# Hybrid encoder trunk: score maxima from half-height matmuls, two key blocks at a time

## The chip, the cores and the metric

The kernel runs on one core of a Trainium2 chip. The metric is the device time of one execution in microseconds (us), as the median of several runs. TensorE (PE) does the matmuls, VectorE (DVE) and ScalarE (ACT) the element-wise work that reads PSUM, GpSimd (POOL) element-wise work between SBUF tiles, and SyncE (SP) issues the DMAs.

## The reference

One layer of an encoder in float32 is applied to two sequences, a prompt of 256 tokens and a sample of 2048, with the same weights. Its parts:

```python
h = rms_norm(x, norm_mix_g)
q, k, v, x_br, y_br = split(h @ w_in)            # 8 query heads, 2 key/value heads of 64
q, k = rope(rms_norm(q)), rope(rms_norm(k))      # per head
s = (q * 64 ** -0.5) @ k.T                       # every query against every key
attn = softmax(s, axis=-1) @ v                   # each key/value head serves 4 query heads
rec = recurrent_group(x_br, y_br)                # gated linear recurrence, both directions
x = x + concat([attn, rec]) @ w_out
x = x + square(relu(rms_norm(x, norm_mlp_g) @ w_up)) @ w_down
y = rms_norm(x, norm_final_g)
```

The softmax must be that of the exact scores; which number is subtracted before the exponential doesn't change it, so long as nothing overflows.

## The kernel before

**Precision.** Every float32 operand of a large matmul is held as two parts, a high one rounded to the array's float32r format and a low one, the rest. A product is the sum of three matmuls: high by high, high by low, low by high (`mm3`, L201 to L204).

**Stages.** The first stage (to some 600 us) does the input projection for all tokens, the recurrence, and the prompt's attention. The second is the region of the changed code: the sample's attention runs beside the output projection and MLP of the prompt and then of the four sample segments of 512 tokens. The MLP of a segment (`mlp`) is the main stream of matmuls, 12 at a time; after each 12 it calls `tick()`, which lets the attention generator take one step (six steps in five ticks, `faster`). The attention is done at some 2500 us, during the third sample segment; the last segment runs without it.

**Attention.** It works in 32 units: 4 segments x 4 query tiles x 2 key/value heads. A unit has 512 query columns (one head, 512 tokens) and 2048 keys of one key/value head. Three SBUF tiles hold all keys and values of the sample: k1 with the high part of the keys in rows 0 to 63 and the low part in rows 64 to 127, k2 with the high part again in rows 0 to 63 and a row of ones as row 64, and vv. A unit has two query tiles: qd holds the high part of the queries twice (rows 0 to 63 and 64 to 127), ql the low part in rows 0 to 63 and, as row 64, minus the maximum of each query. So two matmuls give the scores minus the maxima: k1 by qd (L974: high by high plus low by high) and k2 by ql (L975: high by low, and ones by minus the maxima).

`guard(u)` prepares unit u. It issues the loads of qd for unit u + 1 (`load_q`, three buffers) and of ql for unit u (`load_ql`, two buffers), and then finds the maxima: for each of 4 key blocks of 512 and each of 4 query blocks of 128, one matmul of qd by k1 (L870, with the queries as the weights, so that a row of the result is a query) and one VectorE reduction over it (L871), one of these per step. A reduction over the 4 blocks (L876), four transposes with one column of weights (L880) and a ScalarE copy (L881) then put minus the maxima into row 64 of ql. The maxima's results, the transposes and the sums of `finish` share two PSUM buffers (tag aux).

`values(u)` takes 16 chunks of 128 keys: scores (L974, L975) into one of two PSUM buffers, exp (L982), a copy to the high part (L984), the low part (L986, VectorE), a running sum (L990, POOL), and three chunks later the products with the values (L979, L980). `attention()` runs `guard(u + 1)` beside `values(u)`.

**Order.** No engine's order is written out by hand. The instructions of the whole program are traced first, and a planner then places them on each engine by a simulated timeline: of what is ready it takes what was traced first. The order that it finds is fixed in the program; an engine waits at the head of its order. Where an instruction waits in the plan, later ones go ahead of it.

Of the kernel before, what the change touches and what calls it, by code (L numbers as in the profile page):

```python
# [12 lines left out]
F32 = mybir.dt.float32  # L13
FR = mybir.dt.float32r
AF = mybir.ActivationFunctionType
ALU = mybir.AluOpType
AX = mybir.AxisListType
PSUM = bass.MemoryType.PSUM

P = 128  # L20
# [3 lines left out]
DEC = 2048  # L24
T = SEQ + DEC
NT = 512
# [25 lines left out]
def f32(ap):  # L52
    return ap.bitcast(F32)
# [23 lines left out]
def trunk(ctx, tc, xT, w_in, w_out, w_up, w_down, vecs, wa, wx, cos, sin, outT):  # L77
    nc = tc.nc
    mm = nc.tensor.matmul
    act = nc.scalar.activation  # L80
# [8 lines left out]
    def loadr(out, src):  # L89

        load(f32(out), src)
# [7 lines left out]
    def dtile(shape, name):  # L99
        return dram.tile(shape, F32, name=name, tag=name)  # L100

    def ctile(shape, name, dt=F32):
        return const.tile(shape, dt, name=name, tag=name)
# [15 lines left out]
    k_d = {r: dtile([2, P, n], f"k_d{r}") for r, n in (("p", SEQ), ("s", DEC))}  # L119
# [8 lines left out]
    class WStream:  # L128
# [16 lines left out]
        def load(self, end):  # L145
            while self.at[0] < end:
                i = self.at[0]
                hi, _, first = self.saved[i]
                if first or hi is None:
                    self.f[i] = self._tile("wf", F32, i)  # L150
                    load(self.f[i], self.srcs[i])
                self.at[0] += 1
# [70 lines left out]
    for key in keys:  # L223
        if key[0] == "i":
            w, e = w_in[key[1]], key[2]
        elif key[0] == "o":
            w, e = w_out[key[1]], key[2]
        else:
            (kind, g, f), e = key
            w = w_up[g * G + f] if kind == "u" else w_down[g, f]  # L230
# [6 lines left out]
    nb = (len(srcs) - n1) // len(segs)  # L237
# [10 lines left out]
    for i in range(2):  # L248
        o = ctile([P, P], f"ones_{i}", FR)
# [7 lines left out]
    def load_keys(r, k1, k2, o, n):  # L257
        for k, i in ((k1[0:64], 0), (k1[64:128], 1), (k2[0:64], 0)):
            loadr(k[:, :, o:o + n], k_d[r][i, :, o:o + n].rearrange("(a p) n -> p a n", a=2))
# [12 lines left out]
    with ExitStack() as c1:  # L272
# [461 lines left out]
        for hf in range(2):  # L734
            for ii, m in enumerate((order_s, order_t)[hf]):
                i = len(order_p) + hf * len(order_s) + ii
# [67 lines left out]
    with ExitStack() as c2:  # L804
        banks[0] = itertools.cycle(("m0", "m1"))
        sm = c2.enter_context(tc.tile_pool(name="m2", bufs=1))
        kvp = c2.enter_context(tc.tile_pool(name="kv", bufs=1))
        qp = c2.enter_context(tc.tile_pool(name="q2", bufs=2))
# [2 lines left out]
        ps_s = c2.enter_context(tc.tile_pool(name="pss", bufs=2, space=PSUM))  # L811
        ps_x = c2.enter_context(tc.tile_pool(name="psx", bufs=1, space=PSUM))

        kv_s = [kvp.tile([P, 2, DEC], FR, tag="k1", name="k1"), kvp.tile([65, 2, DEC], FR, tag="k2", name="k2"),
                kvp.tile([P, DEC // P, 320], FR, tag="vv", name="vv2")]
        nc.gpsimd.memset(f32(kv_s[1][64:65]), 1.0)

        nc.gpsimd.memset(f32(kv_s[2][:, :, 128:192]), 1.0)

        def load_kv():  # L820
            for o in range(0, DEC, NT):
                load_keys("s", *kv_s[:2], o, NT)
                yield
            for o in range(0, DEC // P, 4):
                for kv in range(2):
                    loadr(kv_s[2][:, o:o + 4, 192 * kv:192 * kv + P], v_d["s"][:, o:o + 4, kv])
                yield
# [3 lines left out]
        for r, _, _ in segs[1:]:  # L831
            for j in range(4):
                for kv in range(2):
                    rows = slice(64 * kv, 64 * kv + 64)
# [3 lines left out]
        def qview(ap, nj):  # L838
            return ap.rearrange("p (j n) -> p j n", j=nj) if nj > 1 else ap

        def load_q(u):
            _, _, _, q, _, nj = units[u]
            qd = qp.tile([P, NT], FR, tag="qd", name="qd", bufs=3)
            loadr(qview(qd[0:64], nj), q[0])
            loadr(qview(qd[64:128], nj), q[0])
            return qd

        def load_ql(u):
            _, _, _, q, _, nj = units[u]
            ql = qp.tile([65, NT], FR, tag="ql", name="ql2")  # L850
            loadr(qview(ql[0:64], nj), q[1])
            return ql

        qt = {}
# [1 line left out]
        def guard(u):  # L856

            (k1, _, _), nk, kv, _, _, _ = units[u]
            if u + 1 < len(units):
                qt[u + 1] = load_q(u + 1)  # L860
            qd = qt[u]
            ql = load_ql(u)
            qt[u] = (qd, ql)
            w = min(nk, NT)
            nb = nk // w
            mx = sb.tile([P, 4, 4], F32, tag="mx", name="mx", bufs=2)
            for b in range(nb):
                for i in range(4):
                    s = ps_x.tile([P, NT], F32, tag="aux", name="s_mx", bufs=2)
                    mm(s[:, :w], qd[:, i * P:(i + 1) * P], k1[:, kv, b * w:(b + 1) * w], start=True, stop=True)  # L870
                    nc.vector.tensor_reduce(mx[:, i, b:b + 1], s[:, :w], axis=AX.X, op=ALU.max)  # L871
                    yield
            m4 = mx[:, :, 0]
            if nb > 1:
                m4 = sb.tile([P, 4], F32, tag="m4", name="m4", bufs=2)
                nc.vector.tensor_reduce(m4, mx[:, :, :nb], axis=AX.X, op=ALU.max)  # L876
            yield
            pm = ps_x.tile([P, NT], F32, tag="aux", name="pm", bufs=2)
            for i in range(4):
                nc.tensor.transpose(pm[0:1, i * P:(i + 1) * P], m4[:, i:i + 1], ident)  # L880
            act(ql[64:65, :], pm[0:1, :], AF.Copy, scale=-1.0)  # L881

        def finish(u, accs, o_sb, sd):

# [51 lines left out]
        def attention():  # L936

            tail = []
            qt[0] = load_q(0)
            yield from guard(0)  # L940
            yield
            for u, (kvt, nk, kv, _, _, _) in enumerate(units):
                nkc = nk // P
                k1, k2, vv = kvt
                qd, ql = qt.pop(u)
                g = guard(u + 1) if u + 1 < len(units) else iter(())
                acc = sb.tile([P, NT], F32, tag="acc2", name="acc2", bufs=2)
                po = ps_x.tile([P, NT], F32, tag="o", name="po")
                pq = ps_m.tile([P, NT], F32, tag="m2", name="pq")
                tail.append(values(u, po, pq, acc, vv, kv, nkc, qd, ql, k1, k2))  # L950
                i = 0
                while i < nkc or g is not None:
                    i += 1
                    if g is not None and next(g, tail) is tail:
                        g = None
                    for v in list(tail):
                        if next(v, tail) is tail:
                            tail.remove(v)
                    yield
            while tail:  # L960
                for v in list(tail):
                    if next(v, tail) is tail:
                        tail.remove(v)
                yield
# [218 lines left out]
        for m in range(KC):  # L1183
            ws.kept[len(srcs) - KC + m] = [t.rearrange("p a n -> p (a n)")[:, NT * m:NT * m + NT] for t in kv_s[::2]]
        spawn(load_kv())
        spawn(faster(attention(), EVERY))
        with ExitStack() as c3:
# [95 lines left out]
```

## Time and profile before

| | |
|---|---|
| median of 3 runs (lowest to highest) | 3201.34 us (3199.52 to 3202.33) |
| the profiled execution | 3204.86 us |
| its span, first to last instruction | 3203.1 us |
| mean granted TensorE clock | 0.966 of full speed |
| busy: PE, weight loads, DVE, ACT, POOL | 94%, 76%, 57%, 54%, 45% of the span |
| DMA | 598.98 MB, mean 187 GB/s |

The profile records every instruction with its start and its duration. A matmul's duration is its latency: matmuls overlap in the array, so the cost of one in a full stream is the distance from its start to the next one's. Weight loads (PEld) run beside the matmul before them. A wait is put down to the instruction whose end released it. Times of rows count from the start of the span. The tiles k1 and k2 both carry the name k in the rows.

### The profile page before, as it was taken

To read this page: it belongs to the slowest core of one execution; us is meant where nothing else is said; L and a number is where in the kernel's file an instruction comes from. 1 tells how busy PE (TensorE), PEld (TensorE's weight loads), DVE (VectorE), ACT (ScalarE), POOL (GpSimd) and SP (SyncE) were. 2 spreads that over 40 slices of the span, in tenths; PEclk is the share of its full clock that TensorE was granted. 3 is DMA by queue.
4 is the path that set the end of the run, shared out by engine and by line. 5 is a ranking of instruction groups with operands and counts; after the bars stand their busy time and mean duration, and the time that the engine had idled before them with its cause. 6 is when DMAs were issued, how large, how long until landed. Compare 5 with 4: busy or idle time off the path is not lost.

```text
span 3203.1 us, 41975 instructions
## 1 busy us (share of the span) xinstructions
PE 3009.3 (94%) x13646; PEld 2431.3 (76%) x13646; DVE 1823.7 (57%) x2602; ACT 1720.3 (54%) x2988; POOL 1438.2 (45%) x1117
## 2 busy tenths in 40 slices
PE   6699899678999899999999999999999999899998
PEld 5577677566888588888887888888878888778887
DVE  8878776699787754555556555555573311121114
ACT  5465666455666566555556655555566333343333
POOL 4436633577888654334356434433654201411104
PEclk7799999788999899999999999999999999999999
DMA  7656455888766554444456544444664655766554
GB/s 255 200 177 225 158 182 187 257 270 248 236 219 208 170 190 130 148 137 130 148 170 226 166 141 137 139 142 134 218 208 154 189 189 188 261 230 188 188 189 148
DMA packets 346044, 598.98 MB, mean 187 GB/s; under 512 B 44128, under 2 KB 77152, under 8 KB 345824
## 3 DMA queue, kind: packets, MB, share of 16 engines
q1 hardware_dynamic: 345824, 596.30, 58.0%
q8 instruction: 107, 1.75, 0.2%
q14 instruction: 113, 0.93, 0.1%
HBM read 474.52 MB, written 121.63 MB: 186 GB/s over the span
## 4 chain that ended last, share of the span: by engine, by line
PE 68%; DVE 7%; DMA 5%; ACT 3%; issue 2%; POOL 1%; SPq 1%; DVEq 0%; ACTq 0%; POOLq 0%
PE ps_d L204 8%; PE ps_d L202 8%; PE ps_d L203 8%; PE ps_u L204 8%; PE ps_u L203 8%; PE ps_u L202 8%; PE s_t L974 3%; PE s_t L975 3%; PE pq L980 3%; PE po L979 3%; PE s_mx L870 3%; PE ps_o L203 1%; PE ps_o L202 1%; PE ps_o L204 1%; DVE mx L871 1%
## 5 line engine op out<-in xcount | busy, mean ns | idle before, releaser
L990 POOL TENSOR_TENSOR acc<-acc,ph 128x512 f32<-128x512 f32 x448 | 598.8, 1337 | 534.1 <-ACT ph L984 521.6
L168 ACT CAST wh<-wf 128x512 fp32r<-128x512 f32 x712 | 440.2, 619 | 720.7 <-PE ps_d L203 296.2
L986 DVE TENSOR_TENSOR pl<-s_t,ph 128x512 fp32r<-128x512 f32 x512 | 349.6, 684 | 278.6 <-ACT ph L984 274.6
L204 PE MATMUL ps_u<-h2h,wl 128*128 128x512 f32 (+1 forms) x1280 | 479.4, 375 | 7.2 <-DMA wl<-wl_d 3.7
L202 PE MATMUL ps_u<-h2h,wh 128*128 128x512 f32 (+1 forms) x1280 | 478.4, 374 | 0.8 <-DVE xr L1013 0.8
L203 PE MATMUL ps_u<-h2l,wh 128*128 128x512 f32 (+1 forms) x1280 | 478.9, 374 | 0.0
L982 ACT ACTIVATE s_t<-s_t 128x512 f32<-128x512 f32 x512 | 298.1, 583 | 327.5 <-PE s_t L975 310.7
L202 PE MATMUL ps_d<-uh,wh 128*128 128x512 f32 (+1 forms) x1248 | 466.1, 373 | 2.1 <-ACT rl L1031 0.8
L204 PE MATMUL ps_d<-uh,wl 128*128 128x512 f32 (+1 forms) x1248 | 465.8, 373 | 2.2 <-DVE wl L177 1.3
L203 PE MATMUL ps_d<-ul,wh 128*128 128x512 f32 (+1 forms) x1248 | 465.3, 373 | 0.3 <-DVE ul L1035 0.2
L871 DVE TENSOR_REDUCE mx<-s_mx 128x1 f32<-128x512 f32 x512 | 344.1, 683 | 210.5 <-PE s_mx L870 208.8
L1033 POOL TENSOR_TENSOR rl<-rl 128x512 f32<-128x512 f32 (+1 forms) x160 | 159.2, 995 | 626.9 <-ACT uh L1032 620.5
L1146 DVE TENSOR_TENSOR y<-y,ps_d 128x512 f32<-128x512 f32 (+1 forms) x272 | 170.5, 627 | 323.3 <-PE ps_d L204 321.0
L984 ACT ACTIVATE ph<-s_t 128x512 fp32r<-128x512 f32 x512 | 304.7, 597 | 27.7 <-POOL acc L990 2.0
L1035 DVE TENSOR_TENSOR ul<-rl,uh 128x512 fp32r<-128x512 f32 (+1 forms) x160 | 145.9, 912 | 289.3 <-POOL rl L1033 289.2
L204 PEld LDWEIGHTS ps_u<-h2h,wl 128*128 128x128 f32 x1280 | 243.4, 190 | 57.4 <-DMA wl<-wl_d 5.0
L202 PEld LDWEIGHTS ps_u<-h2h,wh 128*128 128x128 f32 x1280 | 243.4, 190 | 50.9 <-DVE xr L1013 1.4
L203 PEld LDWEIGHTS ps_u<-h2l,wh 128*128 128x128 f32 x1280 | 243.3, 190 | 48.3 <-issue 0.5
L202 PEld LDWEIGHTS ps_d<-uh,wh 128*128 128x128 f32 x1248 | 236.4, 189 | 53.0 <-ACT rl L1031 2.2
L204 PEld LDWEIGHTS ps_d<-uh,wl 128*128 128x128 f32 x1248 | 236.1, 189 | 50.1 <-DVE wl L177 2.3
L203 PEld LDWEIGHTS ps_d<-ul,wh 128*128 128x128 f32 x1248 | 236.3, 189 | 48.0 <-DVE ul L1035 1.2
L202 PE MATMUL ps_in<-hh,wh 128*128 128x512 f32 (+1 forms) x560 | 220.8, 396 | 44.1 <-DVE wh L168 16.4
(281 smaller groups left out, 5704.2 us busy)
## 6 DMA issues: line engine op xcount, KB each, us to landing
wl<-wl_d SPq DMA_DIRECT2D x624, 256.0 KB, 2.7
wf<-in_w_up_dram SPq DMA_DIRECT2D x320, 256.0 KB, 3.0
wf<-in_w_down_dram SPq DMA_DIRECT2D x320, 256.0 KB, 3.0
wl_d<-wl SPq DMA_DIRECT2D x172, 256.0 KB, 3.0
wf<-in_w_out_dram SPq DMA_DIRECT2D x80, 256.0 KB, 4.0
wh<-wh_d SPq DMA_DIRECT2D x56, 256.0 KB, 3.4
x<-in_xT_dram SPq DMA_DIRECT2D x32, 256.0 KB, 4.8
qd<-q_ds SPq DMA_DIRECT2D x64, 128.0 KB, 3.0
```

The lines of the kernel that those rows point to most:

```text
L168: self.copy(i)(tile_, self.f[i])
L202: mm(ps, wh, xh, start=first, stop=False)
L203: mm(ps, wh, xl, start=False, stop=False)
L204: mm(ps, wl, xh, start=False, stop=last)
L871: nc.vector.tensor_reduce(mx[:, i, b:b + 1], s[:, :w], axis=AX.X, op=ALU.max)
L982: act(s, s, AF.Exp)
L984: act(ph, s, AF.Copy)
L986: tt(pl, s, f32(ph), op=ALU.subtract)
L990: gtt(acc, acc, f32(ph), op=ALU.add)
L1033: gtt(e[:, :n], e[:, :n], e[:, :n], op=ALU.mult)
L1035: tt(ul[:, f, :n], e[:, :n], f32(uh[:, f, :n]), op=ALU.subtract)
L1146: tt(y[:, :n], y[:, :n], ps[:, :n], op=ALU.add)
```

## The change

The scores' operands are laid out anew. k1 now holds the high part of the keys in both halves of its rows; k2 holds the low part in rows 64 to 127 and zeros in rows 0 to 63, but for a row 0 of ones. qd holds the high part of the queries in rows 0 to 63 and the low part in rows 64 to 127. ql holds the high part in rows 64 to 127, zeros in rows 0 to 63, and minus the maxima in row 0. The two matmuls of the scores (L974, L975 of the kernel before, unchanged in the code) give the same three products; k2 and ql now have 128 rows in place of 65. The tiles of ql are two fixed ones, filled with zeros once, in place of two rotating buffers.

The maxima are now those of the high parts' product alone. Key blocks are taken two at a time: rows 0 to 63 of qd by rows 0 to 63 of k1 for block b, and rows 64 to 127 of ql by rows 64 to 127 of k1 for block b + 1, each into a PSUM buffer of its own, then the two reductions, then two steps without work. The keys' loads of two blocks are issued in one step.

```diff
-        kv_s = [kvp.tile([P, 2, DEC], FR, tag="k1", name="k1"), kvp.tile([65, 2, DEC], FR, tag="k2", name="k2"),
+        kv_s = [kvp.tile([P, 2, DEC], FR, tag="k1", name="k1"), kvp.tile([P, 2, DEC], FR, tag="k2", name="k2"),
                 kvp.tile([P, DEC // P, 320], FR, tag="vv", name="vv2")]
-        nc.gpsimd.memset(f32(kv_s[1][64:65]), 1.0)
+        nc.gpsimd.memset(f32(kv_s[1][0:64]), 0.0)
+        nc.gpsimd.memset(f32(kv_s[1][0:1]), 1.0)
+
+        q2s = [qp.tile([P, NT], FR, tag=f"q2{i}", name="q2", bufs=1) for i in range(2)]
+        for t in q2s:
+            nc.gpsimd.memset(f32(t[0:64]), 0.0)
...
             for o in range(0, DEC, NT):
-                load_keys("s", *kv_s[:2], o, NT)
-                yield
+                for t, i in ((kv_s[0][0:64], 0), (kv_s[0][64:128], 0), (kv_s[1][64:128], 1)):
+                    loadr(t[:, :, o:o + NT], k_d["s"][i, :, o:o + NT].rearrange("(a p) n -> p a n", a=2))
+                if o % (2 * NT):
+                    yield
...
             loadr(qview(qd[0:64], nj), q[0])
-            loadr(qview(qd[64:128], nj), q[0])
+            loadr(qview(qd[64:128], nj), q[1])
             return qd
...
-            ql = qp.tile([65, NT], FR, tag="ql", name="ql2")
-            loadr(qview(ql[0:64], nj), q[1])
+            ql = q2s[u % 2]
+            loadr(qview(ql[64:128], nj), q[0])
             return ql
...
-            for b in range(nb):
+
+            for b in range(0, nb, 2):
                 for i in range(4):
-                    s = ps_x.tile([P, NT], F32, tag="aux", name="s_mx", bufs=2)
-                    mm(s[:, :w], qd[:, i * P:(i + 1) * P], k1[:, kv, b * w:(b + 1) * w], start=True, stop=True)
-                    nc.vector.tensor_reduce(mx[:, i, b:b + 1], s[:, :w], axis=AX.X, op=ALU.max)
+                    ss = [ps_x.tile([P, NT], F32, tag="aux", name="s_mx", bufs=2) for _ in range(2)]
+                    for e, t in enumerate((qd, ql)):
+                        rows = slice(64 * e, 64 * e + 64)
+                        mm(ss[e], t[rows, i * P:(i + 1) * P], k1[rows, kv, (b + e) * w:(b + e + 1) * w],
+                           start=True, stop=True)
+                    for e in range(2):
+                        nc.vector.tensor_reduce(mx[:, i, b + e:b + e + 1], ss[e], axis=AX.X, op=ALU.max)
+                    yield
                     yield
...
-            act(ql[64:65, :], pm[0:1, :], AF.Copy, scale=-1.0)
+            act(ql[0:1, :], pm[0:1, :], AF.Copy, scale=-1.0)
```

## Rows read from the trace of the kernel before

**Rows 1.** Windows: us; PE, PEld, DVE, ACT, POOL busy (instructions); clock, DMA share, GB/s.
```profile
590.00:800.00 210.00, 159.69 (x769) 127.58 (x770) 186.27 (x234) 113.72 (x214) 142.78 (x106) 0.82 0.89 271
800.00:1030.00 230.00, 223.97 (x1490) 200.17 (x1489) 182.79 (x279) 156.96 (x304) 194.30 (x155) 1.00 0.68 225
1030.00:1100.00 70.00, 55.59 (x216) 38.86 (x215) 52.59 (x81) 41.53 (x75) 52.88 (x52) 0.83 0.47 155
1100.00:2440.00 1340.00, 1336.16 (x5767) 1073.82 (x5768) 767.14 (x1122) 777.31 (x1362) 611.74 (x479) 1.00 0.50 160
```

**Rows 2.** The chain that ended last, share of the span by engine.
```profile
PE 68%; DVE 7%; DMA 5%; ACT 3%; issue 2%; POOL 1%; SPq 1%; DVEq 0%; ACTq 0%; POOLq 0%
```

**Rows 3.** Group of L871: count, busy us, mean ns, idle before it, what ended that.
```profile
L871 DVE TENSOR_REDUCE mx<-s_mx 128x1 f32<-128x512 f32 x512 | 344.1, 683 | 210.5 <-PE s_mx L870 208.8
```

**Rows 4.** Timeline of PE: start us, duration us, line, operation.
```profile
1200.28 0.40 PE L980 MATMUL pq<-pl,vv 128*128 128x512 f32 x1
1200.51 0.40 PE L870 MATMUL s_mx<-k,qd 128*128 128x512 f32 x1
1200.75 0.39 PE L203 MATMUL ps_u<-h2l,wh 128*128 128x512 f32 x1
```

**Rows 5.** Windows of L870 alone: us; PE busy, PEld busy (instructions); as rows 1.
```profile
800.00:1030.00 230.00, 29.34 (x78) 13.90 (x77) 1.00 0.68 225
...
1100.00:2440.00 1340.00, 135.97 (x344) 65.04 (x344) 1.00 0.50 160
```

**Rows 6.** Timeline of the weight loads, between matmuls of 256 columns.
```profile
604.63 0.19 PEld L203 LDWEIGHTS ps_o<-cat,wh 128*128 128x128 f32 x1
604.75 0.19 PEld L204 LDWEIGHTS ps_o<-cat,wl 128*128 128x128 f32 x1
```

**Rows 7.** Timeline of PE around one transpose.
```profile
1211.09 0.39 PE L980 MATMUL pq<-pl,vv 128*128 128x512 f32 x1
1211.32 0.27 PE L880 MATMUL pm<-ident,m 128*1 128x128 f32 x1
1211.34 0.48 PE L870 MATMUL s_mx<-k,qd 128*128 128x512 f32 x1
1211.66 0.40 PE L202 MATMUL ps_d<-uh,wh 128*128 128x512 f32 x1
```

**Rows 8.** Timeline of PE: first L870 of two units, a last L975.
```profile
1875.09 0.48 PE L870 MATMUL s_mx<-k,qd 128*128 128x512 f32 x1
...
1898.68 0.40 PE L975 MATMUL s_t<-ql,k 65*128 65x512 f32 x1
...
2375.12 0.48 PE L870 MATMUL s_mx<-k,qd 128*128 128x512 f32 x1
```

**Rows 9.** Timeline of SP: the loads of ql for these two units.
```profile
1900.06 0.54 SPq L91 DMA_DIRECT2D ql<-q_ds  x1
...
2384.86 0.45 SPq L91 DMA_DIRECT2D ql<-q_ds  x1
```

**Rows 10.** Tile ql: its DMAs from issue to landing.
```profile
DMA to landing us min/median/max: 1.9/3.1/6.1
```

**Rows 11.** ACT's waits for weights (us, times, longest); the group of its casts.
```profile
ACT wh L168 <- DMA wf<-in_w_down_dram: 38.1, 21, 4.6
ACT wh L168 <- DMA wf<-in_w_up_dram: 20.8, 16, 4.4
...
L168 ACT CAST wh<-wf 128x512 fp32r<-128x512 f32 x712 | 440.2, 619 | 720.7 <-PE ps_d L203 296.2
```

**Rows 12.** Timeline of POOL: the fill of k2, a later idle time in brackets.
```profile
577.08 3.51 POOL L816 MEMSET k<- 1x4096 f32 x1
...
591.20 1.27 POOL L177 TENSOR_TENSOR wl<-wf,wh 128x512 fp32r<-128x512 f32 x1 [4.78 <-ACT wh L168]
```

**Rows 13.** PE's waits from 1100 to 2440 us (us, times, longest).
```profile
PE s_mx L870 <- DVE mx L871: 4.0, 2, 2.5
PE ps_u L204 <- DMA wl<-wl_d: 1.1, 1, 1.1
```

## The prediction

> **What bounds the kernel now.** I read the busy time by stretch first, then the chain of waits, then the matmuls of the changed lines one by one. From 1100 to 2440 us TensorE is busy 1336.16 of 1340 us and starts 5767 matmuls, one every 0.232 us; from 800 to 1030 it is busy 223.97 of 230 us [rows 1]. In both the granted clock is 1.00, the 2.4 GHz level. From 590 to 800 us it is busy only 159.69 of 210 us at a clock of 0.82, while VectorE is busy 186.27 us and the DMA engines 0.89 of the time; from 1030 to 1100 us the chain exp, copy, subtraction of the attention alone sets the pace [rows 1]. The chain that ended last gives TensorE 68% and VectorE 7% [rows 2]. So a TensorE slot saved is a slot gained in the two full stretches and worth little outside them.
>
> The line that changes, the maxima's matmul (L870), runs 512 times, once for each reduction [rows 3], and is recorded with 0.40 us, but that is latency: its neighbours start 0.23 us before and after it [rows 4]. I price it at 0.233 us, all 512 at 119 us. Of the 512, 78 and 344 lie in the two full stretches, 422 in all [rows 5]. The maxima's reductions (L871, 512 of 683 ns) stay as they are and wait for the matmul, not it for them: 208.8 us of their idle time ended on it [rows 3], while from 1100 to 2440 us TensorE waited for them only twice, 4.0 us [rows 13].
>
> **The change part by part.** My sum goes against the profiled execution, 3204.86 us (span 3203.1, so 1.8 us lie around it); it stands 3.5 us above the median of 3201.34, and I shift the result by that.
>
> *Two matmuls of 64 rows in place of two of 128.* The count stays 512, in 256 pairs; 211 of them are in the full stretches (422 / 2). Only if the second of a pair runs beside the first is anything saved. The trace has no half-array matmul, so I bound it. At best the second is free: 0.233 us a pair. At worst (with no drain, see the rivals) it runs behind the first: 0. What may spoil the overlap is the weights: loads can follow each other after 0.12 us even though each is recorded with 0.19 [rows 6]. If both are in before the preceding matmul ends (2 x 0.12 = 0.24 us against 0.233), the pair costs one slot. If the second load only starts with the first matmul, as each load in the trace starts with the matmul before it, the pair costs 0.12 + 0.233 = 0.353 us in place of 0.466 and saves 0.113. I take the middle of these two, 0.17 us.
>
> *Does going to a half array and back cost something?* The trace has one other change of shape, the transposes with one column of weights. One of them between two full matmuls: from L980 at 1211.09 to L202 at 1211.66 is 0.57 us, two full slots (0.466) and 0.10 for the transpose, its next load included [rows 7]. There is no room for an emptying of the array, whose tail is 0.40 - 0.233 = 0.16 us, twice. I take nothing, and keep 0.32 us per visit as the upper end. The Trainium skill says otherwise (TensorEngine Tiling (Array Packing), Tiling Modes): a change of tiling mode, not just of tile, drains TensorE. By that rule the sum would be the drain rival below; the one-column transposes here don't show it, and no run so far shows it for rows.
>
> *The wait that the change adds.* The second matmul of a pair reads the queries from rows 64 to 127 of ql, where the first reads qd. qd is loaded one unit ahead, but ql has two buffers and is loaded only when the unit two before has done its last L975. Now nothing needs it until the maxima are finished; after the change the first pair does. How early do the maxima start? In the unit whose first L870 is at 1875.09, the buffer's last reader runs at 1898.68 and the load is issued at 1900.06; in the last unit the first L870 is at 2375.12 and the issue at 2384.86 [rows 8, 9]: 25.0 and 9.7 us, 17 on average, and 3.1 us to landing [rows 10], 20 in all. With 344 L870 in 1340 us a pair is due every 7.8 us [rows 1, 5], so two to three of the eight pairs of a unit are due before ql is there. The first matmul of a pair then goes alone, the second is late, and the order of the rest closes up through two PSUM buffers, each held for a matmul and a reduction (0.40 + 0.683 = 1.1 us): about one more pair. I take four of eight pairs as split and four as side by side: 128, of them 105 in the full stretches (128 x 422/512). A split pair costs what it costs now. Gain: 105 x 0.17 = 18 us. Ends: 0 pairs (0 us) and all 211 (211 x 0.233 = 49 us).
>
> The maxima are not late for their user by this: the first score matmul of a unit comes after the last of the unit before, some 60 us after ql is free (a unit takes 16 x 3.9 us), and eight pairs at 2 x 1.1 us need 18.
>
> *What that wait costs when it is met.* TensorE's order is fixed, so a late ql stops every matmul behind it, MLP and attention alike. The order was written for some landing time; what a landing after it costs is seen best on ScalarE, whose casts wait for freshly loaded weights: 21 times 38.1 and 16 times 20.8 us, 1.6 us each, among 712 casts [rows 11], or 0.08 us per cast. For 26 units in the full stretches (422 / 16) I take twice that, 0.15 us, since ql waits behind the two loads of qd on SP: 4 us. Ends: 0, and 1.6 us every time, 42 us.
>
> *The rest.* L975 with 128 rows in place of 65: 0, since a row of 65 already takes 0.40 us like those of 128 [rows 4, 8]. POOL gets a second fill of 4096 elements (3.51 us as the one it has) and two of 512 (3.51 x 512 / 4096 = 0.44 us each): 4.4 us, before its idle 4.78 us at 591 [rows 12]; hidden, and without that cover 4.4 us in a stretch that ACT and the DMA engines pace. DMA bytes and counts stay (three loads a unit, twelve for the keys); the keys of two blocks are issued together: 0 to 3 us once, I take 1.
>
> Sum: -18 + 4 + 1 = -13 us, 3192 for the profiled execution, **3188 us** for the median.
>
> The Trainium skill (TensorE: Matmul & The Clock Gate, Part 3) gives a pack of row tiles the time of one matmul and about 4 ns for each further one; as an estimate from that page the 105 pairs would save 24 us in place of 18. Nothing in this trace shows a pack.
>
> **The rivals.**
> 1. *All pairs run side by side*, because ql is free earlier (a quicker attention lags less) or the second matmul draws the first to it. For it: the two PSUM buffers are nearly always free [rows 13]. Against: the 25 us of [rows 8, 9]. 211 pairs x 0.17 to 0.233 = 36 to 49 us: 3152 to 3165.
> 2. *No overlap*: the half-array matmuls run one after the other, or the pairs come apart in TensorE's order. Then the waits alone remain: 3197 to 3208.
> 3. *Slower: TensorE stands at its head for ql.* Place: the first upper-half matmul of each unit. Price: 1.6 us [rows 11] in 26 units is 42 us, less the 18: 3225; with the whole 4.5 us from L975 to landing, 117 us. It decides from 18 / 26 = 0.7 us per unit on. Against it: in the full stretch TensorE waited for DMA once, 1.1 us, but nothing there is needed so soon after its load.
> 4. *Slower: the array empties at each change to half and back.* 422 - 105 = 317 visits x 0.32 = 101 us, less 18: 3285. It decides from 0.06 us per visit on. Against it: [rows 7].
>
> **How the numbers follow.** Forecast 0.40 (3178 to 3197), rivals 0.15, 0.17, 0.15 and 0.13. I call under 0.2% (6.4 us) no change, about what a measurement of this kernel can tell. Faster: most of 0.40, 0.15 and a little of the second rival, 0.55. Same: 0.19. Slower: rivals 3 and 4 with their small sizes left out, 0.26. The range 3150 to 3228 leaves out the drain, the upper half of rival 3 and the last of rival 1; it holds about 0.8. The forecast's own range is 3178 to 3197.
>
> **What would show it.** Right: L870 rows of 64 x 128, pairs that start within some 0.12 us of each other and a next matmul 0.25 to 0.35 us after the first; in each unit the first L870 alone, then a gap of 10 to 25 us in that line, then a quick series, then pairs; TensorE's wait for DMA at L870 under 10 us in all; VectorE's 344 us of L871 unchanged. Wrong: upper-half matmuls that start 0.23 us after the lower ones (rival 2), matmuls behind a half-array one that start 0.3 us or more late (rival 4), idle TensorE ended by the ql load (rival 3), or no gap at all in a unit's L870 (rival 1).

## The result, and the profile after

The changed kernel takes 3337.18 us (median; 3334.77 to 3343.44) where the kernel before took 3200.43 in the same comparison: a ratio of 1.0433, 95% interval 1.0413 to 1.0454. That is 137 us slower. The forecast was 3188, in a range of 3150 to 3228: wrong in sign.

The first view is the busy time by stretch, in the same columns and the same stretches as [rows 1].

```profile
590.00:800.00 210.00, 163.86 (x744) 118.57 (x744) 177.47 (x224) 107.74 (x207) 144.74 (x108) 0.83 0.87 267
800.00:1030.00 230.00, 230.00 (x1418) 190.05 (x1418) 167.16 (x267) 155.50 (x290) 178.89 (x145) 1.00 0.64 214
1030.00:1100.00 70.00, 62.12 (x287) 43.10 (x285) 50.75 (x80) 42.70 (x80) 59.17 (x57) 0.96 0.43 140
1100.00:2440.00 1340.00, 1333.32 (x5261) 950.78 (x5260) 696.15 (x1032) 705.50 (x1230) 549.86 (x434) 1.00 0.45 145
```

TensorE is still counted as busy all the time from 1100 to 2440 us, and the clock is still the 2.4 GHz level, but in the same 1340 us it starts 5261 matmuls in place of 5767. A full TensorE that does less: the matmuls themselves have become dearer. The chain of waits says the same: TensorE's share rises from 68% [rows 2] to 76% while every other engine's falls or stays.

```profile
PE 76%; DMA 4%; DVE 4%; issue 2%; ACT 1%; POOL 1%; SPq 1%; DVEq 0%; ACTq 0%; POOLq 0%
```

Where the time goes is seen by taking the same MLP matmul (the k-th of L202) in both traces and subtracting its starts. The changed kernel is 2.9 us early where the kernel before is at 582 us, ahead of the first maxima, 16 us late where the kernel before is at 1191 us, 134 us late at 2440 us, and 133 us late at the end. All of it lies where maxima run; none behind them.

So the next view is the timeline around one maxima matmul of the changed kernel, first PE, then PEld (the weight loads). L881 is the matmul that was L870; L884 is its reduction.

```profile
1804.34 0.39 PE L993 MATMUL po<-ph,vv 128*128 128x512 f32 x1
1804.57 0.40 PE L203 MATMUL ps_o<-cat,wh 128*128 128x512 f32 x1
1804.90 0.50 PE L881 MATMUL s_mx<-k,q 64*128 64x512 f32 x1
1805.33 0.50 PE L204 MATMUL ps_o<-cat,wl 128*128 128x512 f32 x1
1805.66 0.40 PE L988 MATMUL s_t<-qd,k 128*128 128x512 f32 x1
1805.89 0.40 PE L989 MATMUL s_t<-q,k 128*128 128x512 f32 x1
```
```profile
1804.35 0.19 PEld L203 LDWEIGHTS ps_o<-cat,wh 128*128 128x128 f32 x1
1804.89 0.18 PEld L881 LDWEIGHTS s_mx<-k,q 64*128 64x128 f32 x1 [0.36 <-issue]
1805.32 0.19 PEld L204 LDWEIGHTS ps_o<-cat,wl 128*128 128x128 f32 x1 [0.25 <-issue]
1805.43 0.19 PEld L988 LDWEIGHTS s_t<-qd,k 128*128 128x128 f32 x1
```

Three intervals are longer than the 0.233 us of [rows 4]: from L203 to the half-array matmul 0.33, from there to L204 0.43, from L204 to L988 0.33. The weight loads show why. Normally the load of the next weights starts with the matmul ahead (L203's load at 1804.35 beside L993 at 1804.34). The load of 64 rows waits until 1804.89, right at its own matmul, and the load of 128 rows behind it waits until 1805.32, right at its own. Neither is hidden, and neither waits for another engine ("issue").

Two halves that do stand side by side look like this:

```profile
1319.70 0.40 PE L989 MATMUL s_t<-q,k 128*128 128x512 f32 x1
1320.03 0.49 PE L881 MATMUL s_mx<-k,q 64*128 64x512 f32 x1
1320.03 0.50 PE L881 MATMUL s_mx<-k,qd 64*128 64x512 f32 x1
1320.46 0.50 PE L203 MATMUL ps_d<-ul,wh 128*128 128x512 f32 x1
1320.81 0.39 PE L204 MATMUL ps_d<-uh,wl 128*128 128x512 f32 x1
```

```profile
1320.03 0.18 PEld L881 LDWEIGHTS s_mx<-k,q 64*128 64x128 f32 x1 [0.37 <-PE pq L994]
1320.03 0.18 PEld L881 LDWEIGHTS s_mx<-k,qd 64*128 64x128 f32 x1
```

The second costs nothing (both loads start at once, and it starts 0.003 us after the first), but the visit as a whole costs the same three long intervals. A visit is one stay at the half array: a matmul of 64 rows, or several with no full-height one between them. The table below is worked out from the traces: medians of the start-to-start intervals of TensorE from 1200 to 2500 us, for this kernel, the kernel before and the experiments further on. "Into" is the interval up to the first matmul of the visit, "within" up to its second, "out" up to the first matmul behind it, "next" the one after that. "Over" is their sum less 0.233 us for each interval.

```
kernel, kind of visit           visits  into   within  out    next   over
before, 128 rows alone             297  0.233          0.233  0.230   0.00
changed, 64 rows alone             278  0.326          0.428  0.339  +0.39
changed, two halves overlapped      18  0.327  0.003   0.428  0.339  +0.165
pairs_together, two halves         153  0.327  0.003   0.428  0.337  +0.16
two_in_a_row, same half twice      160  0.326  0.335   0.323  0.339  +0.39
before_64_rows, 64 rows alone      284  0.326          0.428  0.339  +0.39
before_65_rows, 65 rows alone      291  0.233          0.235  0.234   0.00
extra_64_cols, 64 columns, then 128 160 0.234  0.232   0.231  0.231   0.00
extra_64_rows, 64 rows, then 128   156  0.325          0.428  0.337  +0.39
```

The sum is closed by this: from 1200 us to the end of the maxima (2565 us) there are 292 visits of one and 19 of two, 292 x 0.394 + 19 x 0.165 = 118 us, where the subtraction of the traces gives 134 - 16 = 118.

What stays as it was: the reductions (against [rows 3]) and TensorE's waits, whose largest at the changed line are these. TensorE stood for the late query tile (DMA q) once, 2.5 us, between 1030 and 1100 us, and not at all in the two full stretches.

```profile
L884 DVE TENSOR_REDUCE mx<-s_mx 128x1 f32<-128x512 f32 x512 | 347.7, 686 | 295.9 <-PE s_mx L881 294.1
```
```profile
PE s_mx L881 <- DVE mx L884: 18.0, 16, 7.7
...
PE s_mx L881 <- DMA qd<-q_ds: 10.0, 1, 10.0
...
PE s_mx L881 <- DMA q<-q_ds: 2.5, 1, 2.5
```

### The profile page after: what moved, and what is told of

Read it like the earlier page. It is cut to its first block, busy times and chain, and to the rows that moved or that the text cites. A ratio compares the mean times of both kernels' runs of the same rounds, so it can differ in the third digit from the quotient of the medians.

```text
span 3336.3 us, 41979 instructions
## 1 busy us (share of the span) xinstructions
PE 3158.5 (95%) x13646; PEld 2391.5 (72%) x13646; DVE 1806.7 (54%) x2602; ACT 1726.2 (52%) x2988; POOL 1438.4 (43%) x1120
## 4 chain that ended last, share of the span: by engine, by line
PE 76%; DMA 4%; DVE 4%; issue 2%; ACT 1%; POOL 1%; SPq 1%; DVEq 0%; ACTq 0%; POOLq 0%
PE ps_u L204 8%; PE ps_u L202 8%; PE ps_u L203 8%; PE ps_d L202 8%; PE ps_d L204 8%; PE ps_d L203 8%; PE s_mx L881 6%; PE po L993 4%; PE s_t L988 3%; PE s_t L989 3%; PE pq L994 3%; PE ps_o L202 2%; PE ps_o L203 2%; PE ps_o L204 2%; PE ps_in L202 1%
## 5 line engine op out<-in xcount | busy, mean ns | idle before, releaser
L884 DVE TENSOR_REDUCE mx<-s_mx 128x1 f32<-128x512 f32 x512 | 347.7, 686 | 295.9 <-PE s_mx L881 294.1
L202 PE MATMUL ps_u<-h2h,wh 128*128 128x512 f32 (+1 forms) x1280 | 484.6, 379 | 6.1 <-DVE xr L1027 4.8
L204 PE MATMUL ps_u<-h2h,wl 128*128 128x512 f32 (+1 forms) x1280 | 485.5, 380 | 3.0 <-DMA wl<-wl_d 2.1
L203 PE MATMUL ps_u<-h2l,wh 128*128 128x512 f32 (+1 forms) x1280 | 483.9, 378 | 0.6 <-DVE h2l L1029 0.6
L202 PE MATMUL ps_d<-uh,wh 128*128 128x512 f32 (+1 forms) x1248 | 471.1, 377 | 1.0 <-ACT wh L168 0.6
L204 PE MATMUL ps_d<-uh,wl 128*128 128x512 f32 (+1 forms) x1248 | 468.5, 376 | 0.4 <-DMA wl<-wl_d 0.2
L203 PE MATMUL ps_d<-ul,wh 128*128 128x512 f32 (+1 forms) x1248 | 468.7, 376 | 0.0
L202 PEld LDWEIGHTS ps_u<-h2h,wh 128*128 128x128 f32 x1280 | 243.3, 190 | 64.4 <-issue 10.7
L204 PEld LDWEIGHTS ps_u<-h2h,wl 128*128 128x128 f32 x1280 | 243.2, 190 | 61.9 <-issue 12.6
L1049 DVE TENSOR_TENSOR ul<-rl,uh 128x512 fp32r<-128x512 f32 (+1 forms) x160 | 136.7, 854 | 275.3 <-POOL rl L1047 275.2
L203 PEld LDWEIGHTS ps_u<-h2l,wh 128*128 128x128 f32 x1280 | 243.3, 190 | 55.7 <-issue 10.7
L202 PEld LDWEIGHTS ps_d<-uh,wh 128*128 128x128 f32 x1248 | 235.7, 189 | 59.1 <-issue 9.7
L204 PEld LDWEIGHTS ps_d<-uh,wl 128*128 128x128 f32 x1248 | 235.3, 189 | 53.8 <-issue 8.8
L203 PEld LDWEIGHTS ps_d<-ul,wh 128*128 128x128 f32 x1248 | 235.7, 189 | 52.3 <-issue 8.8
L202 PE MATMUL ps_in<-hh,wh 128*128 128x512 f32 (+1 forms) x560 | 221.7, 398 | 43.6 <-DVE wh L168 16.4
```

What stands on the lines that cost most here:

```text
L202: mm(ps, wh, xh, start=first, stop=False)
L203: mm(ps, wh, xl, start=False, stop=False)
L204: mm(ps, wl, xh, start=False, stop=last)
L884: nc.vector.tensor_reduce(mx[:, i, b + e:b + e + 1], ss[e], axis=AX.X, op=ALU.max)
```

## The experiments

Three theories stood at the start. A: the array pays for each change between 64 and 128 rows. B: the wait for ql costs the time, by splitting the pairs or by stopping TensorE. C: the new layout costs it (a second score matmul of 128 rows, fills, loads).

**full_height: the new layout without a half array.**

```
-   for e, t in enumerate((qd, ql)): mm(ss[e], t[rows, ...], k1[rows, kv, ...])
+   for e, t in enumerate((qd, ql)): mm(ss[e], qd[:, ...], k1[:, kv, ...])
```

> The changed kernel with its new operand layout, but each of the 512 maxima matmuls takes all 128 rows of qd (high and low queries) against the doubled high keys, so no matmul of 64 rows is left and the maxima need no ql. (The maxima are then of (high + low queries) x high keys.) Theory A, the array pays for each change between 64 and 128 rows (0.39 us per visit in the trace of the changed kernel: 0.33, 0.43, 0.34 us in place of three slots of 0.233): the whole 137 us go, 3195 to 3207 us, ratio 0.998 to 1.002. Theory B, the wait for ql and the split order cost the time: also 3190 to 3207. Theory C, the new layout costs it (128 rows in the second score matmul, fills, loads): 3325 to 3340.

Measured: 3198.81 us, ratio 0.9999 (0.9987 to 1.001). C falls: the layout, the fills and the loads cost nothing that can be measured.

**full_height_wait: the wait for ql kept.**

```
-   mm(ss[e], t[rows, ...], k1[rows, kv, ...])
+   mm(ss[e], t[:, ...], k1[:, kv, ...])
+   nc.gpsimd.memset(f32(ql[0:1]), 0.0)        # in load_ql
```

> The same with 128 rows, but the second matmul of each pair reads the ql tile, as in the changed kernel, so the wait for ql's buffer and load stays (row 0 of ql, which held an older unit's maximum, is filled with zeros by POOL ahead of the load). Theory A (change of rows): 3195 to 3210, as without the wait. Theory B (the wait for ql): 3310 to 3340.

(The maxima of the odd blocks are then of high queries x high keys.) Measured: 3187.25 us, ratio 0.9966 (0.9953 to 0.9979), below what every theory said. B falls: with the same wait and no half array nothing is lost, and TensorE stood for ql 1.1 us.

```profile
L881 PE MATMUL s_mx<-k,qd 128*128 128x512 f32 x256 | 106.7, 417 | 27.4 <-DVE mx L884 15.8 <-DMA qd<-q_ds 11.4
L881 PE MATMUL s_mx<-k,q 128*128 128x512 f32 x256 | 105.8, 413 | 6.7 <-DVE mx L884 4.2 <-DMA q<-q_ds 1.1 <-ACT q L895 0.7
```

**before_64_rows and before_65_rows: the old kernel, one number changed.**

```
-   mm(s[:, :w], qd[:, i * P:(i + 1) * P], k1[:, kv, ...])
+   mm(s[:, :w], qd[0:64, i * P:(i + 1) * P], k1[0:64, kv, ...])      # or 0:65
```

> The kernel before with one edit: each maxima matmul takes rows 0 to 63 alone (high queries x high keys), one by one as before; no pairs, no ql, no new layout. Theory A: 468 visits in TensorE's order; the changed kernel paid 137 us for 459, 0.298 each net of what lies beside other waits, so +140: 3330 to 3350 us, ratio about 1.044; the matmul starts 0.33 after the one ahead, the next 0.43 after it, the one after that 0.34. Theories B and C: 3195 to 3207, for neither the wait nor the layout is in it.

> The kernel before with one edit: each maxima matmul takes rows 0 to 64, one row more than 64 (high queries x high keys and one row of the low keys). Theory A in the form that the price is for the array's halves and not for the number of rows: 3195 to 3207, slots of 0.233 us as before, as the second score matmul of 65 rows already has. In the form that any matmul of fewer than 128 rows pays: 3330 to 3350.

Measured: 64 rows 3347.94 us, ratio 1.0468 (1.0449 to 1.0488); 65 rows 3190.28 us, 0.9974 (0.9964 to 0.9985), 5 us below the range expected. One row less costs 158 us. The timeline with 65 rows, PE and then PEld, shows the plain slots and a weight load that starts with the matmul ahead (1300.02 beside 1300.01):

```profile
1300.01 0.39 PE L202 MATMUL ps_u<-h2h,wh 128*128 128x512 f32 x1
1300.25 0.40 PE L870 MATMUL s_mx<-k,qd 65*128 65x512 f32 x1
1300.48 0.40 PE L979 MATMUL po<-ph,vv 128*128 128x512 f32 x1
```
```profile
1300.02 0.19 PEld L870 LDWEIGHTS s_mx<-k,qd 65*128 65x128 f32 x1
```

So the price is not for fewer rows as such, for 65 of 128 cost nothing; it is for the half array. Theory A is shown with neither pairs nor the new layout nor the wait in the kernel.

**pairs_together: what the pairs would bring if they stood side by side.**

```
-   ss = [ps_x.tile([P, NT], ..., tag="aux", bufs=2) for _ in range(2)]
+   ss = ps_x.tile([P, 2, NT], ..., tag="aux", bufs=1)
-   for e in range(2): nc.vector.tensor_reduce(mx[:, i, b + e:b + e + 1], ss[e], ...)
+   nc.vector.tensor_reduce(mx[:, i, b:b + 2], ss, ...)
```

The other users of tag aux (the transposes, the sums) take the first half of such a tile, so in this kernel and the next two one tile serves where two buffers did.

> The changed kernel, but the two halves of a pair write one tile of two PSUM banks and one reduction takes both, so the pair gets its banks together and stands side by side in TensorE's order: 233 of the 256 pairs in place of 40, 37 matmuls alone. Theory A: an overlapped pair costs 0.327 + 0.003 + 0.428 + 0.339 = 1.10 us where four full slots cost 0.93, so +0.165; with 0.75 of the price in the open, as in the changed kernel (0.298 of 0.395): (233 x 0.165 + 37 x 0.395) x 0.75 = +40, 3225 to 3255 us. Theory B (what was missing is that the pairs run side by side): 211 pairs x 0.17 to 0.233 saved, 3152 to 3165.

**two_in_a_row** has in addition `enumerate((qd, qd))` and `rows = slice(0, 64)`:

> As pairs_together (one tile of two banks, one reduction), but both matmuls of a pair take rows 0 to 63 of qd, one after the other: 259 visits to the half array, 248 of them of two matmuls that can't overlap. Theory A with the price per visit: 259 x 0.298 = +77, 3265 to 3290 us, and within a visit the second matmul starts 0.23 us after the first. Price per matmul of 64 rows instead: 512 x 0.298, 3340 to 3360. No price (theory B, no wait for ql is left): 3195 to 3207.

**full_together** has that tile and reduction with `qd[:, ...]` and `k1[:, kv, ...]`:

> As pairs_together with its one tile of two banks and one reduction, but with 128 rows from qd in both matmuls: what the tile and the merged reduction do by themselves. Theories A and B: 3190 to 3207 us. If the single two-bank tile costs by itself (matmuls wait for the reduction of the pair ahead): up to 3225, and then the two other runs with that tile are to be read against this one.

Measured: pairs_together 3262.41 us, ratio 1.0212 (1.0194 to 1.023); two_in_a_row 3285.52, 1.0283 (1.0266 to 1.0301); full_together 3203.75, 1.0028 (1.0017 to 1.0039). Even with 233 pairs side by side the change loses, so the forecast's own gain was not there to be had. The price is per visit: two_in_a_row visits the half array 259 times and loses 82 us against full_together, before_64_rows visits it 468 times and loses 150 against before, 0.32 each in both. Inside a visit the second matmul of the same half starts 0.33 us after the first, where 0.23 was expected (one row of the view stands for both), and out of it are 0.32 and 0.34:

```profile
1355.00 0.40 PE L204 MATMUL ps_d<-uh,wl 128*128 128x512 f32 x1
1355.33 0.73 PE L881 MATMUL s_mx<-k,qd 64*128 64x512 f32 x2
1355.99 0.50 PE L202 MATMUL ps_d<-uh,wh 128*128 128x512 f32 x1
1356.33 0.40 PE L203 MATMUL ps_d<-ul,wh 128*128 128x512 f32 x1
```

This places the price more exactly: at the changes, 0.195 us each. The first matmul after a change starts 0.09 late (0.326 into the half array, 0.323 out of it), and the matmul behind that one 0.10 to 0.11 late (0.335 within, 0.339 next). A lone half has both in one interval, 0.233 + 0.09 + 0.10 = 0.43 out of it. The weight loads go with this: by the medians of the traces the first load after a change starts 0.002 us ahead of its own matmul, the second already 0.23 us ahead, as in a full stream. Why the matmul behind is still late is not shown.

pairs_together missed its expectation by 7 us on the slow side. Against full_together it loses 59 us, where 272 visits by the table would give about 233 x 0.165 + 39 x 0.39 = 54 if all of it lay in the open. In this kernel TensorE also thins out at two changes of the MLP's segment, of which the second, the window from 2380 to 2420 us (columns as [rows 1]), puts it about 20 us further behind the kernel before (by the same MLP matmuls): it starts 111 matmuls in 40 us, and the granted clock is 0.83, part of the stretch at each of its two levels (1.2 and 2.4 GHz), after waits of the engine.

```profile
2380.00:2420.00 40.00, 31.52 (x111) 20.49 (x110) 28.04 (x34) 22.01 (x38) 19.51 (x15) 0.83 0.46 161
```

full_together has only the first such place, and both fall back by 27 to 28 us there. By the same MLP matmuls pairs_together lies 37 us behind full_together where the kernel before is at 2301 us, and 58 us where it is at 2380. So some 21 of the 59 us come at the second place and 37 elsewhere, where the visits are; of the 54, then, about two thirds lay in the open, as far as programs that differ in order by some 10 us can tell. Whether the half array has a part in the 21 us was not tried.

**extra_full, extra_64_cols, extra_64_rows: a change of columns against a change of rows.** The kernel before, with 256 more matmuls, in three shapes:

```
+   if b % 2:
+       mm(s[:, :w], qd[:, i * P:(i + 1) * P], k1[:, kv, ...])        # extra_full
+       mm(s[0:64, :w], qd[:, i * P:i * P + 64], k1[:, kv, ...])      # or extra_64_cols
+       mm(s[:, :w], qd[0:64, i * P:(i + 1) * P], k1[0:64, kv, ...])  # or extra_64_rows
    mm(s[:, :w], qd[:, i * P:(i + 1) * P], k1[:, kv, ...])
```

> The kernel before, and ahead of each maxima matmul of the blocks 1 and 3 the same matmul once more (256 more, each overwritten by the one behind it): 128 rows and 128 columns of weights. The measure for the two runs beside it: 256 slots of 0.233 us, 60 us, of which 0.82 to 1 lie in full stretches: 3246 to 3258 us by every theory.

> The same 256 extra matmuls with 64 columns of weights in place of 128 (128 rows; queries 0 to 63 of each block). If only a change of rows costs: as extra_full within 0.3%, slots of 0.233 us, 3243 to 3260. If any change of the tile costs 0.298 net per visit: 256 x 0.298 = 76 more, 3320 to 3335.

> The same 256 extra matmuls with 64 rows (0 to 63) in place of 128 (all 128 columns). Theory A: 256 visits x 0.298 = 76 us more than extra_full, 3320 to 3335, with intervals of 0.33, 0.43 and 0.34 us around each. Theories B and C: as extra_full.

Measured: extra_full 3225.8 us, ratio 1.0095 (1.0078 to 1.0111); extra_64_cols 3232.51, 1.0104 (1.0083 to 1.0124); extra_64_rows 3325.27, 1.0404 (1.0386 to 1.0422). Columns cost nothing that can be told from a full matmul (the two intervals overlap). Rows cost 99.5 us over it, 0.39 for each of the 256 visits: the interval sum of the table (expected were 76). Over extra_64_cols it is 93 us, 0.36 a visit, so the agreement is no finer than that. The absolute level of extra_full was missed, 28 us for 256 slots in place of 49 to 60, and with it that of extra_64_cols, 35 us. By the same MLP matmuls it is 14 us ahead of the kernel before where that one is at 873 us; the rest of the gap was not pursued.

The weight loads of the 64 columns start with the matmul ahead, as in a full stream (1309.71 beside 1309.70):

```profile
1309.70 0.39 PE L981 MATMUL po<-ph,vv 128*128 128x512 f32 x1
1309.93 0.39 PE L871 MATMUL s_mx<-k,qd 128*64 128x512 f32 x1
1310.16 0.40 PE L872 MATMUL s_mx<-k,qd 128*128 128x512 f32 x1
1310.40 0.39 PE L204 MATMUL ps_u<-h2h,wl 128*128 128x512 f32 x1
```
```profile
1309.71 0.14 PEld L871 LDWEIGHTS s_mx<-k,qd 128*64 128x64 f32 x1
1309.94 0.19 PEld L872 LDWEIGHTS s_mx<-k,qd 128*128 128x128 f32 x1
```

In extra_64_rows the same place reads:

```profile
1304.92 0.50 PE L871 MATMUL s_mx<-k,qd 64*128 64x512 f32 x1
1305.35 0.50 PE L872 MATMUL s_mx<-k,qd 128*128 128x512 f32 x1
1305.68 0.39 PE L202 MATMUL ps_d<-uh,wh 128*128 128x512 f32 x1
```

**full_height_wait_again: the version that beats both.**

> The kernel of full_height_wait, which came out 0.34% faster than before (0.9953 to 0.9979), in five rounds on another chip: whether it beats both kernels. If that was the chip: 0.999 to 1.001. If it is the order of the matmuls in this program: 0.995 to 0.998, 3182 to 3192 us against 3198.

Measured: 3188.49 us, ratio 0.9978 (0.997 to 0.9986). It is faster than before in both comparisons, by 0.2 to 0.3%. What its gain is made of was not settled. By the MLP matmuls full_height_wait is ahead by 27 us where the kernel before is at 1317 us, and at 1816 us only by 18; in this second run it is 22 and 14. Several programs that do the same amount of TensorE work differ by this much (before_65_rows 0.9974, full_height 0.9999, full_together 1.0028), so the order of the matmuls is the likely cause, argued and not shown.

## Why the prediction was wrong, step by step

**What bounds the kernel: right.** The full stretches are where the change counts, at the same granted clock of 1.00.

**The step that failed: "Does going to a half array and back cost something? I take nothing."** It costs 0.39 us per visit: 0.09 into it, 0.20 out of it, 0.11 at the matmul behind. The evidence was read beyond what it shows. The one-column transposes of [rows 7] change the columns of the tile and keep its 128 rows; extra_64_cols shows that columns are free, extra_64_rows that rows are not. [rows 7] said nothing on rows, and the 65-row matmul L975 [rows 8] sits on the full-array side of an edge that before_64_rows and before_65_rows place between 64 and 65. The Trainium skill (TensorEngine Tiling (Array Packing), Tiling Modes) says that a change of tiling mode drains TensorE; the traces agree so far that a change of rows costs time, 0.39 us for the two changes of a visit, and show no cost for 128 to 64 columns of weights. That the array empties is not shown: the half-array matmul at 1804.90 starts 0.07 us ahead of the recorded end of L203 (1804.57 + 0.40), and recorded ends are modelled. With the price at 0.39 the forecast's own sum turns round.

**The upper end of that step was too low as well, and so was the drain rival.** Rival 4, at 0.13, had the right place, a price at each change to the half array and back; the emptying that it names as the reason stays open. Its price was two pipeline tails, 0.32 us; the weight loads, which no longer start a matmul ahead, were not in it. Its 317 visits left out the overlapped pairs, as if they saved; an overlapped pair loses 0.165. Its 3285 us fell short by 52.

**Pairs side by side: the count was wrong, the mechanism of the split right.** In every unit the first matmul goes alone, and in units 10 to 31 (counted from 0) the second half of its pair follows 5 to 22 us later, when ql has landed: unit 13 starts at 1304.29, its ql load is issued at 1313.64, its second half runs at 1320.03. But the order did not close up after one more pair. The late half mostly stands beside the first half of the next pair (as at 1320.03), and from there on the two halves of a pair stay apart for the rest of the unit: of 256 pairs, 4 have their own halves side by side, and 30 second halves run beside the first of the next pair, 22 of these as the first second half of a unit. In pairs_together, where both halves write one tile, 237 pairs have their own halves side by side, so the shift comes with the separate tiles and reductions; why it lasts was not tried further.

**0.17 us saved per pair: wrong, and not for the reason named as its risk.** The weights of both halves are in at once and the overlap is full. The Trainium skill (TensorE: Matmul & The Clock Gate, Part 3) puts about 4 ns on each further tile of a pack; the traces agree, with 3 to 4 ns. It is the two changes of rows around the pair that eat the slot that it saves.

**The wait for ql: right in kind, small.** 4 us were set for it in the full stretches; TensorE stood 2.5 us for ql, none of it there, and full_height_wait shows no loss. Rival 3 is ruled out.

**The rest at nothing to 1 us: right.** full_height carries the new layout, the fills and the changed loads at 0.9999.

## What to carry to other kernels

- Before packing matmuls of 64 rows, count the visits to the half array and not the slots saved: each visit between full-height matmuls cost 0.39 us here, an overlapped pair saves 0.233. As an estimate from the table's intervals, two pairs in one visit against 1.40 us at full height would take 1.33 with the way out of two_in_a_row (0.323) and 1.44 with that of an overlapped pair (0.428), so the sign is open; three would take at most 1.77 against 1.86 and gain. That needs six PSUM buffers of one result each and was not run.
- Evidence for a cheap change of shape holds only for the dimension that it changes. Among full-height matmuls a row count of 65 (before_65_rows) or 128 with zeros (the second score matmul of full_height) cost a plain slot here, and a lone matmul of 64 rows did not.
- A TensorE that is busy all the time can still lose throughput: compare the number of matmuls per stretch, and the intervals between their starts, before the busy time.

## What the runs showed of the hardware that was not expected

- Between 64 and 65 rows lies a step of 158 us for 512 matmuls (3347.94 against 3190.28 us), with the same 512 columns moved.
- At a change between 128 and 64 rows the weight load starts only at its own matmul (1804.89 for 1804.90, 1805.32 for 1805.33), in both directions, and the slot behind that matmul is longer too: 0.335 us to a second matmul of the same 64 rows, 0.339 us to the second one of 128 rows. Two of different halves start 0.003 us apart.
